# Hybrid encoder layer with 16 experts: the first expert gathered by itself, and its weights laid out block by block in the first ring slots

## The chip, the core and the metric

The kernel runs on one core of a Trainium2 chip. The metric is the device time of one execution in microseconds (us); the kernel before takes 1386.49 us as the median of 3 runs (1386.35 to 1389.76).

## What is computed

One encoder layer on 512 tokens of width 1024, all in float32: a trunk (an mLSTM branch and a differential attention branch, gated, projected and added to x), then a mixture of 16 experts in which each expert chooses its 64 best tokens, then a norm. The change lies at the seam between trunk and experts.

```python
def expert_choice_ffn(h, w_router, w_gate, w_up, w_down):
    cap = EC_CAPACITY * S // N_EXPERTS            # 64
    aff = jax.nn.softmax(jnp.einsum('bsd,de->bse', h, w_router), axis=-1)
    g, idx = lax.top_k(aff.transpose(0, 2, 1), cap)
    xe = h[bidx, idx]
    hid = (jax.nn.silu(jnp.einsum('becd,edf->becf', xe, w_gate))
           * jnp.einsum('becd,edf->becf', xe, w_up))
    ye = jnp.einsum('becf,efd->becd', hid, w_down) * g[..., None]
    return jnp.zeros_like(h).at[bidx, idx].add(ye)
```

Each expert has three weight matrices of 1024 x 2048 or 2048 x 1024, 8.39 MB each; the 16 experts have 402.7 MB.

## The kernel before

**The seam.** The trunk ends with the router and the choice of tokens: eight rounds of max and match-replace on VectorE (DVE) give each expert's threshold, two masks `gt_` and `eq_` (lines 931, 932) say which tokens are above or at it, and matmuls with a triangle of ones (`before`, lines 938 to 944) count how many chosen tokens stand ahead of each. The result is `slot` (line 948): the place of each token in each expert's list of 64. Dummy matmuls by `keep_warm` (line 159, `zps<-ident`) stand in the program's order on TensorE (PE): 28 beside the eight rounds, and `WARM2` = 7 ahead of the counting matmuls.

**Gather.** The 64 tokens of an expert are picked by a matmul with a one-hot matrix `ohr`, scaled by the token's norm. `gather(p)` does this for a pair of experts at once: per block of 128 features four matmuls (line 997) have `xn`, 128 x 128, as the stationary operand and 128 columns of `ohr` (64 of each expert) as the moving one. ScalarE (ACT) and DVE in turn bring the result from PSUM into `xe` (lines 1001, 999). A pair has 8 such blocks, b = 0 to 7. Before expert 0 the DVE makes `ohr` for the pair with three large operations (lines 983, 987); later pairs use small ones, half of them on GpSimd (POOL; line 991).

**An expert.** The gate pass and the up pass have 8 feature blocks each (line 1045, `pgate<-w,xe` and `pup<-w,xe`); a block is 4 matmuls of 512 columns, and reads 1 MB of weights. Then come Silu (ACT, line 1213), a product (DVE, line 1225), transposes of the hidden activations (`hid_T`, lines 1076 to 1080), and the down pass (line 1111). The order on PE and on SyncE (SP) is the program's: expert 0 does gate and up in turn, piece by piece, with the gather between (`first_up`); every expert e from 1 on does its gate pass, in which the transposes of expert e-1 lie (and, for an even e, the gather of its pair; for an odd e, the matrices of the scatter, lines 1016 and 1027), then the down pass of e-1, then its up pass.

**The weight ring.** Weights come through 11 slots of 2 MB (`mw`). The list `PIECES` says in which order: 192 pieces of 2 MB, that is two blocks of gate or up, or a quarter of a down matrix. SP issues one DMA per piece, in this order; a piece that goes into a used slot waits on SP until the PE has done the last matmul of the slot's old piece, and all later pieces wait behind it. The first 11 pieces (the 16 blocks of expert 0, and 6 of the 8 gate blocks of expert 1) are loaded beside the end of the trunk, as its tiles come free. Three slots are taken out of the ring for other data on their way (`keep`): the slot of expert 0's last up piece holds the scatter's matrices (`mats`). Piece n of the rest and its slot: 11 (expert 1, gate, last) in 0; 12 to 15 (expert 0, down) in 1 to 4; 16 and 17 (expert 1, up) in 5 and 6; 18 and 19 in 8 and 9; 20 (expert 2, gate, first) in 10; 21 in 0.

`sg` (activations of an expert) and `hT` (their transposes) are two tiles of 4 KB per partition of their own.

Of the kernel before, what the change touches and what calls it, by code (L numbers as in the profile page):

```python
# [9 lines left out]
F32 = mybir.dt.float32  # L10
# [8 lines left out]
P = 128  # L19
# [14 lines left out]
NG = 9  # L34
WARM0 = 30
WARM1 = 28
WARM2 = 7
NSLOT = 11

PIECES = [(0, m, j) for j in range(4) for m in ("gate", "up")]  # L40
PIECES += [(e, m, j) for s in range(1, NE + 1)
           for e, m in ((s, "gate"), (s - 1, "down"), (s, "up")) if e < NE
           for j in range(4)]


def _slots():

    keep = {(0, "up", 3): "mats", (1, "down", 3): "acc", (12, "gate", 0): "gf"}
    of, kept, old = list(range(NSLOT)), {}, 0
    for _ in range(NSLOT, len(PIECES)):  # L50
        while PIECES[old] in keep:
            kept[keep[PIECES[old]]] = of[old]
            old += 1
        of.append(of[old])
        old += 1
    return of, kept
# [6 lines left out]
def kernel(  # L63
# [869 lines left out]
    keep_warm(WARM2)  # L933
    cnt = [bank(t, (P, NT, NE)) for t in ("sc", "pv")]

    def before(c, m, first, last):
# [6 lines left out]
    for t in range(NT):  # L943
        pe.matmul(cnt[1], one, gt_[:, t:t + 1].broadcast_to([P, NT, NE]), start=(t == 0), stop=False)
    before(cnt[1], eq_, False, True)
    for i in range(2):
        ve.tensor_tensor(pl2[:, i], msk[:, i], cnt[i], op=OP.mult)
    ve.tensor_add(slot, pl2[:, 0], pl2[:, 1])
# [11 lines left out]

        return mw.tile([P, 4096], dtype, tag=f"w{KEPT[what]}", name=what)

    def slot_for(e, m, j):
        n = npiece[0]
        assert PIECES[n] == (e, m, j)
        npiece[0] += 1
        return mw.tile([P, 4096], F32, tag=f"w{SLOT_OF[n]}", name="w")

# [2 lines left out]

    xe = mm.tile([P, ND, 2 * CAP], F32, name="xe")
    ohr = mm.tile([P, NT, 2 * CAP], F32, name="ohr")
    sg = mm.tile([P, D], F32, name="sg")
    hT_ = mm.tile([P, ND, P], F32, name="hT")
    ga = consts.tile([P, 2, 1], F32, name="ga")
    fs = consts.tile([P, 6, NT], F32, name="fs")

    def gather(p):

        if p == 0:
            o4 = ohr.rearrange("p t (j c) -> p t j c", j=2)
            ve.tensor_tensor(o4, iota.unsqueeze(1).unsqueeze(1).broadcast_to([P, NT, 2, CAP]),
                             slot[:, :, 0:2].unsqueeze(3).broadcast_to([P, NT, 2, CAP]), op=OP.is_equal)
            for t in (0, 2):
                o = ohr[:, t:t + 2]
                ve.tensor_tensor(o, o, rst2[:, t:t + 2].unsqueeze(2).broadcast_to([P, 2, 2 * CAP]), op=OP.mult)  # L987
        for t in range(NT if p else 0):
            for j in range(2):
                e = 2 * p + j  # L990
                (gp if j else ve).tensor_scalar(ohr[:, t, j * CAP:(j + 1) * CAP], iota, slot[:, t, e:e + 1],
                                                rst2[:, t:t + 1], op0=OP.is_equal, op1=OP.mult)
        for b in range(ND):
            pg = pgt((P, 2 * CAP))
            c0 = 256 * (b // 2) + b % 2
            for t in range(NT):
                pe.matmul(pg, xn[t][:, c0:c0 + 255:2], ohr[:, t], start=(t == 0), stop=(t == NT - 1))  # L997
            if b % 2:
                ve.tensor_scalar(xe[:, b], pg, gff[:, b:b + 1], None, op0=OP.mult)
            else:  # L1000
                se.activation(xe[:, b], pg, AF.Copy, scale=gff[:, b:b + 1])  # L1001
            yield

    def scatter_mats(p):
# [27 lines left out]
    def up_bank(tag):  # L1032
        return pm.tile([P, 2, 512], F32, tag=tag, name=tag, bufs=1)

    def up_piece(e, m, w, j, pu, ahead, behind):
        half = (e % 2) * CAP
        wt = slot_for(e, m, j)
        sy.dma_start(wt, w[0, e, j * 256:(j + 1) * 256, :].rearrange("(p i) f -> p (i f)", i=2))
        for i in range(2):
            next(ahead, None)  # L1040
            b = 2 * j + i
            for c in range(2):
                for s in range(2):
                    c0 = i * DFF + s * D + c * 512
                    pe.matmul(pu[s * 64:(s + 1) * 64, c], xe[:, b, half:half + CAP], wt[:, c0:c0 + 512],  # L1045
                              start=(b == 0), stop=(b == ND - 1))
                next(behind, None)

    def up_pass(e, m, w, tag, ahead, behind):

        pu = up_bank(tag)
        next(ahead, None)
        for j in range(4):
            up_piece(e, m, w, j, pu, ahead, behind)
        for _ in behind:
            pass
        return pu

    def first_up():

        g, pg, pu = gather(0), up_bank("pgate"), up_bank("pup")
        next(g)
        next(g)
        for j in range(4):
            up_piece(0, "gate", w_gate_e, j, pg, nothing, nothing)
            up_piece(0, "up", w_up_e, j, pu, g, nothing)
        return pg, pu

    def hid_T():
# [135 lines left out]
    for e in range(NE + 1):  # L1205
        b = e - 1
        if e == 0:
            pg, pu = first_up()
        elif e < NE:
            pg = up_pass(e, "gate", w_gate_e, "pgate", nothing if e % 2 else gather(e // 2),  # L1210
                         chain(hid_T(), scatter_mats(b // 2) if e % 2 else nothing))
        if e < NE:
            se.activation(sg, pg.rearrange("p a b -> p (a b)"), AF.Silu)
        if 0 < e < NE:
            down(b)
        if e == NE:
            for _ in hid_T():
                pass
            last_down(b)
        else:  # L1220
            if e:
                pu = up_pass(e, "up", w_up_e, "pup", nothing, scatter(b // 2) if b % 2 else nothing)
# [40 lines left out]
```

## Time and profile before

| | |
|---|---|
| median of 3 runs | 1386.49 us |
| the profiled execution: its time, its span | 1386.85 us, 1384.8 us |
| PE busy | 1300.5 us, 94% |
| DVE, ACT, POOL busy | 412.6, 306.9, 120.8 us |
| bytes moved by DMA | 444.30 MB, mean 321 GB/s |
| mean granted TensorE clock | 0.993 of full speed |
| chain that ended last | PE 65%, DMA 29%, DVE 3%, ACT 2%, issue 1% |

The span runs from the first to the last instruction; the time of the execution has 2.05 us more around it. The trunk takes the first 455 us, the experts the rest. PE's busy share is high throughout, but PE is counted as busy while matmuls are pipelined; which engine sets the pace of the experts is read from the DMA's share and from PE's waits. "Chain that ended last" follows the last instruction back through whatever released each step.

### The profile page before, as it was taken

The page shows a single profiled execution, that of the slowest core. Times are in us where ns is not written, and L with a number is a line of the kernel's source. Part 1 is how long each engine was busy: PE and PEld are TensorE (multiplying, and loading weights), DVE is VectorE, ACT ScalarE, POOL GpSimd, SP SyncE. Part 2 cuts the span into 40 slices and gives each one's busy share as a digit, 9 for nine tenths or more (in the row PEclk, how much of TensorE's full clock was granted, in tenths as well). Part 3 has the DMA queues.
Part 4 walks back from the last instruction along what each step waited for, and adds up shares of the span by engine and source line. Part 5 has one row for each costly group of instructions (what it writes and reads, how often), then busy time and mean ns, then how long its engine had stood idle before and what let it go on. Part 6 is the DMA issues. An engine that isn't in the chain of part 4 may idle for free.

```text
span 1384.8 us, 16485 instructions
## 1 busy us (share of the span) xinstructions
PE 1300.5 (94%) x6762; PEld 723.6 (52%) x6762; DVE 412.6 (30%) x989; ACT 306.9 (22%) x634; POOL 120.8 (9%) x217
## 2 busy tenths in 40 slices
PE   8999999999999999999999997999899799889976
PEld 8988887888888434334333332423333242333435
DVE  5787759753344111111121020120112012001113
ACT  7676646433331010000000100000000000100003
POOL 3010312101201020000000000000000000000001
PEclk9999999999999999999999999999999999999998
DMA  7222242223488799999999999999999999999995
GB/s 202 63 77 77 77 107 61 77 76 106 129 327 344 276 415 430 425 430 428 426 428 428 427 429 425 428 428 428 429 426 428 427 429 427 428 428 428 426 403 178
DMA packets 84312, 444.30 MB, mean 321 GB/s; under 512 B 6176, under 2 KB 53350, under 8 KB 60174
## 3 DMA queue, kind: packets, MB, share of 16 engines
q1 hardware_dynamic: 81966, 438.95, 77.9%
q10 hardware_dynamic: 2240, 4.25, 1.2%
q8 instruction: 53, 0.87, 0.3%
q14 instruction: 21, 0.17, 0.0%
q0 software_dynamic: 32, 0.07, 0.0%
HBM read 441.10 MB, written 2.11 MB: 320 GB/s over the span
## 4 chain that ended last, share of the span: by engine, by line
PE 65%; DMA 29%; DVE 3%; ACT 2%; issue 1%; SPq 0%; DVEq 0%; ACTq 0%
DMA w<-in_w_up_e_dram 26%; PE pgate L1045 13%; PE pup L1045 10%; PE pd L1111 4%; PE zps L301 4%; PE zps L303 4%; PE zps L302 4%; PE pg L997 4%; PE pg L1098 3%; DMA w<-in_w_gate_e_dram 2%; PE pt L1076 1%; PE pn L582 1%; PE pa L1016 1%; PE bank L775 1%; PE zps L611 1%; PE zps L610 1%
## 5 line engine op out<-in xcount | busy, mean ns | idle before, releaser
L1045 PE MATMUL pup<-w,xe 128*64 128x512 f32 x1024 | 240.2, 601 | 35.7 <-DMA w<-in_w_up_e_dram 35.7
L1045 PE MATMUL pgate<-w,xe 128*64 128x512 f32 x1024 | 245.7, 605 | 0.3 <-DMA w<-in_w_gate_e_dram 0.3
L1111 PE MATMUL pd<-w,hT 128*64 128x512 f32 x896 | 198.1, 594 | 16.1 <-DMA w<-in_w_down_e_dram 16.1
L1045 PEld LDWEIGHTS pup<-w,xe 128*64 128x64 f32 x1024 | 65.6, 136 | 175.8 <-issue 114.1
L1111 PEld LDWEIGHTS pd<-w,hT 128*64 128x64 f32 x896 | 62.7, 137 | 149.2 <-issue 115.8
L1093 DVE SCALAR_TENSOR_TENSOR mats<-pd,ga,mats 64x512 fp32r<-64x512 f32 (+2 forms) x36 | 24.9, 690 | 329.2 <-ACT mats L1091 328.7
L1045 PEld LDWEIGHTS pgate<-w,xe 128*64 128x64 f32 x1024 | 64.4, 136 | 100.7 <-issue 88.8
L301 PE MATMUL zps<-hH,sp 128*128 128x512 f32 x256 | 102.0, 398 | 0.8 <-DVE hL L225 0.8
L303 PE MATMUL zps<-hH,sp 128*128 128x512 f32 x256 | 100.0, 391 | 0.0
L302 PE MATMUL zps<-hL,sp 128*128 128x512 f32 x256 | 99.8, 390 | 0.0
L241 DVE TENSOR_TENSOR sp<-raw,sp 128x512 fp32r<-128x512 f32 x114 | 78.1, 688 | 54.3 <-ACT sp L240 51.7
L997 PEld LDWEIGHTS pg<-ohr,xn 128*128 128x128 f32 x512 | 65.2, 198 | 46.5 <-issue 46.5
L240 ACT ACTIVATE sp<-raw 128x512 fp32r<-128x512 f32 x114 | 70.6, 629 | 69.3 <-PE zps L611 27.6
L997 PE MATMUL pg<-ohr,xn 128*128 128x128 f32 x512 | 75.9, 294 | 1.8 <-DVE ohr L987 1.8
L1091 ACT ACTIVATE mats<-pd,ga 64x512 fp32r<-64x512 f32 (+2 forms) x36 | 22.9, 635 | 220.6 <-PE pd L1111 196.9
L1225 DVE TENSOR_TENSOR sg<-sg,pup 128x512 f32<-128x512 f32 x32 | 20.6, 684 | 151.9 <-PE pup L1045 151.9
L1001 ACT ACTIVATE xe<-pg,gff 128x128 f32<-128x128 f32 x32 | 11.8, 367 | 233.5 <-PE pg L997 233.5
L1080 ACT ACTIVATE hT<-pt 128x512 f32<-128x512 f32 x16 | 9.6, 597 | 229.8 <-PE pt L1076 229.8
L1010 POOL TENSOR_SCALAR mats<-iota,slot 128x64 fp32r<-128x64 f32 x64 | 26.7, 444 | 335.6 <-PE pt L1027 328.4
L301 PEld LDWEIGHTS zps<-hH,sp 128*128 128x128 f32 x256 | 48.1, 188 | 10.6 <-POOL sp L275 1.0
L303 PEld LDWEIGHTS zps<-hH,sp 128*128 128x128 f32 x256 | 48.1, 188 | 10.4
L302 PEld LDWEIGHTS zps<-hL,sp 128*128 128x128 f32 x256 | 48.2, 188 | 9.5
(323 smaller groups left out, 1583.7 us busy)
## 6 DMA issues: line engine op xcount, KB each, us to landing
w<-in_w_gate_e_dram SPq DMA_DIRECT2D x64, 2048.0 KB
w<-in_w_up_e_dram SPq DMA_DIRECT2D x64, 2048.0 KB
w<-in_w_down_e_dram SPq DMA_DIRECT2D x60, 2048.0 KB
raw<-in_w_in_dram SPq DMA_DIRECT2D x44, 512.0 KB
raw<-in_w_out_dram SPq DMA_DIRECT2D x8, 512.0 KB
w<-in_w_down_e_dram SPq DMA_DIRECT2D x4, 1024.0 KB
x<-in_x_dram SPq DMA_DIRECT2D x4, 512.0 KB
mb<-mrow_d ACTq DMA_DIRECT2D x4, 512.0 KB
```

The source lines that it names most:

```text
L240: se.activation(sp[:, 0], raw, AF.Copy)
L241: ve.tensor_sub(sp[:, 1], raw, sp[:, 0].bitcast(F32))
L301: pe.matmul(zp, w[:, 1], hT(hH, k), start=(k == 0), stop=False)
L302: pe.matmul(zp, w[:, 0], hT(hL, k), start=False, stop=False)
L303: pe.matmul(zp, w[:, 0], hT(hH, k), start=False, stop=(k == ND - 1))
L997: pe.matmul(pg, xn[t][:, c0:c0 + 255:2], ohr[:, t], start=(t == 0), stop=(t == NT - 1))
L1010: (gp if j else ve).tensor_scalar(oa[:, t, j * CAP:(j + 1) * CAP], iota, slot[:, t, e:e + 1], None, op0=OP.is_equal)
L1045: pe.matmul(pu[s * 64:(s + 1) * 64, c], xe[:, b, half:half + CAP], wt[:, c0:c0 + 512], start=(b == 0), stop=(b == ND - 1))
L1091: se.activation(yb[r, 0, c], src[r], AF.Copy, scale=ga[r, e % 2])
L1093: ve.scalar_tensor_tensor(yb[r, 1, c], src[r], ga[r, e % 2], yb[r, 0, c].bitcast(F32), op0=OP.mult, op1=OP.subtract)
L1098: pe.matmul(pq, oaT[:, v, t], yb[:, i, cols], start=(i == 0), stop=(i == 1))
L1111: pe.matmul(pd[s * 64:(s + 1) * 64], hid_col(q, i), wt[:, i * D + hf * 512:i * D + (hf + 1) * 512], start=(c == 0), stop=(c == 15))
```

## The change

- The first 12 pieces are made of single blocks of 1 MB, two to a slot: (gate 0, up 0), (gate 1, up 1) ... (gate 6, up 6) of expert 0 in slots 0 to 6, then (gate 7 of expert 0, gate 0 of expert 1) in 7, and gate 1 and 2, 3 and 4, 5 and 6 of expert 1 in 8, 9 and 10. Piece 11 is gate 7 of expert 1, alone in slot 0. The slot kept for `mats` is 6. Up 7 of expert 0 goes into a 12th place: the 8 KB per partition of the tile `sh`, which after expert 0 holds `sg` and `hT`. SP issues one DMA of 1 MB for each of these 24 blocks.
- From piece 12 on the list is the old one. The slots of pieces 12 to 16 stay; 17 goes into slot 7 (before: 6); 18, 19, 20 and 21 stay in 8, 9, 10 and 0.
- `gather(0, (0,))` picks the tokens of expert 0 alone (64 moving columns), in the pass of expert 0; `gather(0, (1,))` those of expert 1, in the gate pass of expert 1. Expert 0's one-hot columns are made by four small DVE operations.
- Expert 0 does gate and up block by block: gather block b+1, gate b, up b.
- `WARM2` is 4, and these dummy matmuls come after the counting matmuls.

```diff
-WARM2 = 7
+WARM2 = 4
...
-PIECES = [(0, m, j) for j in range(4) for m in ("gate", "up")]
+BLOCKS = [(0, m, b) for b in range(8) for m in ("gate", "up")][:-1] + [(1, "gate", b) for b in range(8)]
+PIECES = [tuple(BLOCKS[n:n + 2]) for n in range(0, len(BLOCKS), 2)]
+NFIRST = len(PIECES)
...
-    keep = {(0, "up", 3): "mats", (1, "down", 3): "acc", (12, "gate", 0): "gf"}
+    keep = {PIECES[6]: "mats", (1, "down", 3): "acc", (12, "gate", 0): "gf"}
...
-    sg = mm.tile([P, D], F32, name="sg")
-    hT_ = mm.tile([P, ND, P], F32, name="hT")
...
+    for _ in range(NSLOT):
+        first_piece()
+    early[0, "up", 7] = mm.tile([P, DFF], F32, tag="sh", name="wsh", bufs=1)
+    weights(early[0, "up", 7], 0, "up", 7)
...
+    def gather(p, js=(0, 1)):
+
+        for j in js:
+            for t in range(NT):
                 e = 2 * p + j
                 (gp if j else ve).tensor_scalar(ohr[:, t, j * CAP:(j + 1) * CAP], iota, slot[:, t, e:e + 1],
                                                 rst2[:, t:t + 1], op0=OP.is_equal, op1=OP.mult)
+        js = slice(js[0] * CAP, (js[-1] + 1) * CAP)
...
-                pe.matmul(pg, xn[t][:, c0:c0 + 255:2], ohr[:, t], start=(t == 0), stop=(t == NT - 1))
+                pe.matmul(pg[:, js], xn[t][:, c0:c0 + 255:2], ohr[:, t, js], start=(t == 0), stop=(t == NT - 1))
...
-        g, pg, pu = gather(0), up_bank("pgate"), up_bank("pup")
+        g, pg, pu = gather(0, (0,)), up_bank("pgate"), up_bank("pup")
         next(g)
-        next(g)
-        for j in range(4):
-            up_piece(0, "gate", w_gate_e, j, pg, nothing, nothing)
-            up_piece(0, "up", w_up_e, j, pu, g, nothing)
+        for b in range(ND):
+            next(g, None)
+            up_block(0, b, early[0, "gate", b], pg)
+            up_block(0, b, early[0, "up", b], pu)
...
             pg, pu = first_up()
+            sh = mm.tile([P, 2 * D], F32, tag="sh", name="sh", bufs=1)
+            sg, hT_ = sh[:, 0:D], sh[:, D:].rearrange("p (a b) -> p a b", a=ND)
         elif e < NE:
-            pg = up_pass(e, "gate", w_gate_e, "pgate", nothing if e % 2 else gather(e // 2),
+            pg = up_pass(e, "gate", "pgate", gather(0, (1,)) if e == 1 else nothing if e % 2 else gather(e // 2),
                          chain(hid_T(), scatter_mats(b // 2) if e % 2 else nothing))
```

How the order on the engines changes, at three places. The first is PE at the end of the choice of tokens (`tk`: the thresholds, `tri` and `one`: triangle and square of ones, `msk`: the masks). Before:

```order
L927 MATMUL bank<-ident,tk 128x16
L159 MATMUL zps<-ident 128x128 x7
L938 LDWEIGHTS tri
L938 MATMUL bank<-msk,tri 128x64
...
L940 MATMUL bank<-msk,one 128x16
L997 MATMUL pg<-ohr,xn_3779 128x128
```

and now:

```order
L930 MATMUL bank<-ident,tk 128x16
L940 LDWEIGHTS tri
L940 MATMUL bank<-msk,tri 128x64
...
L942 MATMUL bank<-msk,one 128x16
L162 MATMUL zps<-ident 128x128 x4
L1011 MATMUL pg<-ohr,xn_3779 128x64
```

The dummy matmuls no longer stand ahead of the counting ones, and the gather has half the columns. The second place is PE in the gate pass of expert 1, from the last block of expert 0 (`pup`) to the down pass (`pd`). Before:

```order
L1045 MATMUL pup<-w,xe 64x512 x8
L1045 MATMUL pgate<-w,xe 64x512 x6
L1076 MATMUL pt<-ident,sg 128x128 x4
L1045 MATMUL pgate<-w,xe 64x512 x4
L1076 MATMUL pt<-ident,sg 128x128 x4
L1045 MATMUL pgate<-w,xe 64x512 x6
L1016 MATMUL pa<-aff,mats 128x2 x8
...
L1045 MATMUL pgate<-w,xe 64x512 x8
L1111 MATMUL pd<-w,hT 64x512 x32
```

and now its beginning (each gather is four rows of `L1011`, of which one is shown):

```order
L1054 MATMUL pup<-wsh,xe 64x512 x4
L1011 MATMUL pg<-ohr,xn_3779 128x64
...
L1054 MATMUL pgate<-w,xe 64x512 x4
L1011 MATMUL pg<-ohr,xn_3779 128x64
...
L1054 MATMUL pgate<-w,xe 64x512 x2
L1096 MATMUL pt<-ident,sh 128x128 x4
L1054 MATMUL pgate<-w,xe 64x512 x2
L1011 MATMUL pg<-ohr,xn_3779 128x64
...
L1054 MATMUL pgate<-w,xe 64x512 x8
L1131 MATMUL pd<-w,sh 64x512 x32
```

Eight gather blocks have come into this pass, two of them ahead of its first block. The third place is ACT at the end of expert 0. Before:

```order
L1001 ACTIVATE xe<-pg,gff 128x128 x4
L1213 ACT_TABLE_LOAD
L1213 ACTIVATE sg<-pgate 128x1024
L1080 ACTIVATE hT<-pt 128x512
```

and now:

```order
L1015 ACTIVATE xe<-pg,gff 128x64 x4
L1235 ACT_TABLE_LOAD
L1235 ACTIVATE sh<-pgate 128x1024
L1015 ACTIVATE xe<-pg,gff 128x64 x2
L1100 ACTIVATE sh<-pt 128x512
```

Behind the Silu now stands the `xe` of expert 1's first gather block; and the Silu writes the tile that held up 7, so the wait for the last matmul of that block stands ahead of the table load.

## Rows read from the trace of the kernel before

**Rows 1.** The page, busy tenths in 40 slices of 34.6 us:
```profile
PE   8999999999999999999999997999899799889976
DMA  7222242223488799999999999999999999999995
```
**Rows 2.** Windows: stretch, engines' busy us, clock, DMA share, GB/s.
```profile
455.00:469.00 14.00, 13.72 (x68) 7.27 (x70) 1.17 (x4) 0.73 (x2) 0.00 (x0) 0.88 0.40 144
469.00:510.00 41.00, 41.00 (x210) 17.27 (x206) 5.83 (x21) 4.55 (x7) 6.23 (x14) 1.00 0.98 401
510.00:530.00 20.00, 20.00 (x96) 6.75 (x94) 1.50 (x2) 2.67 (x4) 2.81 (x7) 1.00 1.00 417
530.00:1310.00 780.00, 732.86 (x3460) 278.01 (x3458) 110.44 (x228) 58.73 (x96) 33.75 (x72) 1.00 1.01 428
```
**Rows 3.** Timeline of SP's DMA issues: start, us, what (pieces 11, 20, 21).
```profile
462.61 0.33 SPq L1038 DMA_DIRECT2D w<-in_w_gate_e_dram  x1
...
509.10 0.33 SPq L1038 DMA_DIRECT2D w<-in_w_gate_e_dram  x1
...
513.27 0.33 SPq L1038 DMA_DIRECT2D w<-in_w_gate_e_dram  x1
```
**Rows 4.** Chain that ended last, from the thresholds to the first gate block.
```profile
451.36 1.76 PE zps L159 x14
...
453.25 0.46 DVE pl L947 x2
453.73 0.23 DVE slot L948
...
455.28 2.81 PE pg L997 x16
458.09 4.48 PE pgate L1045 x16
```
**Rows 5.** Timeline of DVE: the mask, and small one-hot operations of the next pair.
```profile
451.47 0.22 DVE L931 TENSOR_TENSOR msk<-aff,bank 128x64 bf16<-128x64 f32 x1 [0.39 <-PE bank L927]
...
484.94 0.79 DVE L991 TENSOR_SCALAR ohr<-iota,slot,rst 128x64 f32<-128x64 f32 x3 [8.39 <-PE pg L997]
```
**Rows 6.** Chain, expert 0's pass in its regular part: one period of 4 blocks.
```profile
468.58 3.43 PE pgate L1045 x16
472.01 1.14 PE pg L997 x8
473.15 1.87 PE pup L1045 x8
...
478.03 3.43 PE pgate L1045 x16
```
**Rows 7.** Chain, the gate pass of expert 1 and its end.
```profile
494.34 2.57 PE pgate L1045 x12
496.92 0.68 PE pt L1076 x4
...
502.86 1.88 PE pa L1016 x16
...
506.61 0.59 PE pt L1027 x4
...
513.23 13.73 PE pd L1111 x64
```
**Rows 8.** Timeline of ACT around the Silu of expert 0.
```profile
482.64 0.37 ACT L1001 ACTIVATE xe<-pg,gff 128x128 f32<-128x128 f32 x1 [9.08 <-PE pg L997]
483.02 1.28 ACT L1213 ACT_TABLE_LOAD   x1
490.95 1.02 ACT L1213 ACTIVATE sg<-pgate 128x1024 f32<-128x1024 f32 x1 [6.65 <-PE pgate L1045]
```
**Rows 9.** Windows of 1 us: granted clock is the third number from the end.
```profile
457.00:458.00 1.00, 1.00 (x6) 0.79 (x4) 0.00 (x0) 0.00 (x0) 0.00 (x0) 0.50 0.00 0
...
460.00:461.00 1.00, 1.00 (x6) 0.29 (x4) 0.00 (x0) 0.00 (x0) 0.00 (x0) 1.00 0.00 0
```

More of the change, by code (lines that the diff above doesn't have):

```diff
@@ L36 @@
 WARM1 = 28
-WARM2 = 7
+WARM2 = 4
 NSLOT = 11
-PIECES = [(0, m, j) for j in range(4) for m in ("gate", "up")]
+BLOCKS = [(0, m, b) for b in range(8) for m in ("gate", "up")][:-1] + [(1, "gate", b) for b in range(8)]
+PIECES = [tuple(BLOCKS[n:n + 2]) for n in range(0, len(BLOCKS), 2)]
+NFIRST = len(PIECES)
 PIECES += [(e, m, j) for s in range(1, NE + 1)
-           for e, m in ((s, "gate"), (s - 1, "down"), (s, "up")) if e < NE
+           for e, m in ((s, "gate"), (s - 1, "down"), (s, "up")) if e < NE and (e, m) != (1, "gate")
            for j in range(4)]
 def _slots():
-    keep = {(0, "up", 3): "mats", (1, "down", 3): "acc", (12, "gate", 0): "gf"}
+    keep = {PIECES[6]: "mats", (1, "down", 3): "acc", (12, "gate", 0): "gf"}
     of, kept, old = list(range(NSLOT)), {}, 0
@@ L932 @@
     ve.tensor_tensor(eq_, aff, taus, op=OP.is_equal)
-    keep_warm(WARM2)
     cnt = [bank(t, (P, NT, NE)) for t in ("sc", "pv")]
@@ L945 @@
     before(cnt[1], eq_, False, True)
+    keep_warm(WARM2)
     for i in range(2):
@@ L961, in kept, with slot_for @@
         return mw.tile([P, 4096], dtype, tag=f"w{KEPT[what]}", name=what)
-    def slot_for(e, m, j):
+    def slot_for(*key):
         n = npiece[0]
-        assert PIECES[n] == (e, m, j)
+        assert PIECES[n] == key
         npiece[0] += 1
@@ L973, with weights, first_piece @@
     ohr = mm.tile([P, NT, 2 * CAP], F32, name="ohr")
-    sg = mm.tile([P, D], F32, name="sg")
-    hT_ = mm.tile([P, ND, P], F32, name="hT")
+    def weights(wt, e, m, b, n=1):
+        w = (w_gate_e if m == "gate" else w_up_e)[0, e, b // 2 * 256:(b // 2 + 1) * 256, :]
+        sy.dma_start(wt, w.rearrange("(p i) f -> p (i f)", i=2)[:, b % 2 * DFF:(b % 2 + n) * DFF])
+    early = {}
+    def first_piece():
+        n = npiece[0]
+        wt = slot_for(*PIECES[n])
+        for i, key in enumerate(PIECES[n]):
+            early[key] = wt[:, i * DFF:(i + 1) * DFF]
+            weights(early[key], *key)
+    for _ in range(NSLOT):
+        first_piece()
+    early[0, "up", 7] = mm.tile([P, DFF], F32, tag="sh", name="wsh", bufs=1)
+    weights(early[0, "up", 7], 0, "up", 7)
     ga = consts.tile([P, 2, 1], F32, name="ga")
     fs = consts.tile([P, 6, NT], F32, name="fs")
[L979 to L989, printed above, removed]
+    def gather(p, js=(0, 1)):
+        for j in js:
+            for t in range(NT):
                 e = 2 * p + j
@@ L996, in gather @@
             for t in range(NT):
-                pe.matmul(pg, xn[t][:, c0:c0 + 255:2], ohr[:, t], start=(t == 0), stop=(t == NT - 1))
+                pe.matmul(pg[:, js], xn[t][:, c0:c0 + 255:2], ohr[:, t, js], start=(t == 0), stop=(t == NT - 1))
             if b % 2:
-                ve.tensor_scalar(xe[:, b], pg, gff[:, b:b + 1], None, op0=OP.mult)
+                ve.tensor_scalar(xe[:, b, js], pg[:, js], gff[:, b:b + 1], None, op0=OP.mult)
             else:
-                se.activation(xe[:, b], pg, AF.Copy, scale=gff[:, b:b + 1])
+                se.activation(xe[:, b, js], pg[:, js], AF.Copy, scale=gff[:, b:b + 1])
             yield
@@ L1033, in up_bank, with up_block, up_pass @@
         return pm.tile([P, 2, 512], F32, tag=tag, name=tag, bufs=1)
-    def up_piece(e, m, w, j, pu, ahead, behind):
+    def up_block(e, b, wt, pu, behind=nothing):
         half = (e % 2) * CAP
[L1037 to L1049, printed above, removed]
+        for c in range(2):
+            for s in range(2):
+                c0 = s * D + c * 512
+                pe.matmul(pu[s * 64:(s + 1) * 64, c], xe[:, b, half:half + CAP], wt[:, c0:c0 + 512],
+                          start=(b == 0), stop=(b == ND - 1))
+            next(behind, None)
+    def up_pass(e, m, tag, ahead, behind):
         pu = up_bank(tag)
         next(ahead, None)
-        for j in range(4):
-            up_piece(e, m, w, j, pu, ahead, behind)
+        for b in range(ND):
+            if (e, m) == (1, "gate"):
+                if npiece[0] < NFIRST:
+                    first_piece()
+                wt = early[e, m, b]
+            elif b % 2 == 0:
+                both = slot_for(e, m, b // 2)
+                weights(both, e, m, b, 2)
+                wt = both[:, 0:DFF]
+            else:
+                wt = both[:, DFF:]
+            next(ahead, None)
+            up_block(e, b, wt, pu, behind)
         for _ in behind:
@@ L1059, in first_up @@
     def first_up():
-        g, pg, pu = gather(0), up_bank("pgate"), up_bank("pup")
+        g, pg, pu = gather(0, (0,)), up_bank("pgate"), up_bank("pup")
         next(g)
-        next(g)
-        for j in range(4):
-            up_piece(0, "gate", w_gate_e, j, pg, nothing, nothing)
-            up_piece(0, "up", w_up_e, j, pu, g, nothing)
+        for b in range(ND):
+            next(g, None)
+            up_block(0, b, early[0, "gate", b], pg)
+            up_block(0, b, early[0, "up", b], pu)
         return pg, pu
@@ L1221 @@
             if e:
-                pu = up_pass(e, "up", w_up_e, "pup", nothing, scatter(b // 2) if b % 2 else nothing)
+                pu = up_pass(e, "up", "pup", nothing, scatter(b // 2) if b % 2 else nothing)
             for i in range(2):
```

## The prediction

> **What bounds the kernel now.** First the slices of the page [rows 1]: DMA stands at 9 from the 15th slice (485 us) to the 39th, while PE shows gaps from the 25th (830 us) on. So the weight stream sets the pace there, and it has no hole to its end. Then the windows [rows 2]: over the 780 us from 530 to 1310 it moves 428 GB/s, so a block of 1 MB (1.0486 MB) takes 2.45 us and a piece of 2 MB 4.9 us. Between 455 and 469 the mean is 144 GB/s: all 11 slots are full, so 22 blocks are in, and nothing more is asked for until PE gives a slot back. The first issue after that is at 462.61 [rows 3].
>
> So there is one number to watch: how many blocks have arrived by 530 us, from where the stream never stops. Before, these are 22 + (144 x 14 + 401 x 41 + 417 x 20) / 1048.6 = 22 + 25.56 = 47.56 [rows 2]. Each block more or less at 530 moves the end by 2.45 us, because the pieces that follow are the same in both kernels, and PE waits for them. The question is therefore not when expert 0 is done but when slots come free, and in which order.
>
> **How quickly slots come free.** Before, expert 0 has a period of 9.45 us (468.58 to 478.03) for 4 blocks [rows 6], that is two slots; the stream needs 9.8 us for them. The two are nearly matched, so from 469 to 530 the stream just runs (401 and 417 GB/s), and any delay of PE in this stretch is a delay of the stream. Of the period, a block takes 3.43 / 2 = 1.715, a gather block 1.14, and coming back from it 1.87 - 1.715 = 0.155 [rows 6]: a gather costs 1.295.
>
> **Edits, part by part.**
>
> *Warm-up moved.* On the chain the 7 dummy matmuls stand from 451.36 to 453.12 ahead of the counting [rows 4], though the mask begins at 451.47 and takes 0.22 [rows 5]. Now the counting begins at about 451.8, and `slot` is there about 1.0 earlier, at 452.95 instead of 453.96. One small one-hot operation (0.79 / 3 = 0.26 [rows 5]) takes the place of two large ones, so the gather begins about 453.35 instead of 455.28: 1.9 earlier. Four dummies (4/7 of 1.76 = 1.0) lie beside the DVE's work. The gather's first block is paced by four one-hot operations to 454.3, the second ends at 455.3. The first gate block begins at 455.35 instead of 458.09.
>
> *Clock.* Before, the granted clock falls to 0.50 (1.2 GHz) in the microsecond at 457 and is back at 1.00 (2.4 GHz) at 460 [rows 9], after PE stood idle up to 455.28. Two gather blocks took 2.81 instead of 2 x 1.14, and four blocks 4.48 instead of 3.43 + 0.155 [rows 4, 6]: 1.4 together. Now PE has work through the same stretch, and I take 2.4 GHz; the other end is 1.4 later.
>
> *Half the columns per gather.* No row has a gather of 64 columns. `pa` has the same 128 x 128 stationary tile and only 2 moving columns: 16 records in 1.88 [rows 7], so 8 take 0.94, against 1.14 with 128 columns. A gather of 64 costs between 0.94 and 1.14, with the return between 1.095 and 1.295; I take the middle, 1.2, since 64 lies halfway. Two of them cost 2.4 where one of 1.295 stood: gathering apart adds PE work. By contrast the Trainium skill, page "TensorE: Matmul & The Clock Gate", section "Step-by-step: what each phase is for", calls throughput "purely `N cycles`", one moving column per cycle. By that, a gather of 64 would be half of one of 128, and the sum would come out as in the second rival below.
>
> *Expert 0.* Slot 0 comes free after gate 0 and up 0: 455.35 + 0.155 + 3.43 = 458.95, against 462.57 before (458.09 + 4.48 [rows 4]). Each further slot takes 3.43 + 1.2 = 4.63: 463.6, 468.2, 472.8, 477.5, 482.1 for slots 1 to 5. Slot 6 is kept. Expert 0 ends at 455.35 + 0.155 + 16 x 1.715 + 6 x 1.2 = 490.15 instead of 494.34 [rows 7].
>
> *The 12th place.* Up 7 is one block more in stock. Its DMA waits for `slot` (452.95), and the stream has work up to about there, so it is in by 457. The 12 more issues on SP (0.33 each [rows 3]) are covered by the stream's own time; without that cover they would cost 4.
>
> *Silu.* The table load (1.28) and the Silu (1.02) now start at the end of up 7, and the `xe` of expert 1's first block (0.37) waits behind them [rows 8]: before, the table was loaded at 483.02, while PE worked. With 0.2 for three handovers (my estimate) the first gate block begins at 490.15 + 2.87 = 493.0. The two gather blocks ahead of it would be done by 492.2, so this wait costs 0.8; it lies on PE's path.
>
> *Gate pass of expert 1.* Before it takes 513.23 - 494.34 = 18.89 [rows 7]: 8 blocks 13.72, transposes 2 x 0.68, `pa` 1.88, `pt` 2 x 0.59, and 5 returns of 0.155. Now six gathers come in between (7.2; two were ahead), three of them right behind `pa` or `pt`, which saves returns. Its gates end at 493.0 + 0.155 + 13.72 + 7.2 + 4.42 + 2 x 0.155 = 518.8, not 513.23. Slot 7, which now waits for gate 0 of expert 1, comes free at 494.85. Slots 8, 9 and 10 each have two blocks, two gathers and a transpose pair, `pa` or a `pt` pair: 7.5, 7.7 and 7.0 more, so 502.35, 510.05, 517.1.
>
> **The sum.** A lone piece lands 6.6 after its issue: piece 11, issued at 462.61, has 2.02 of its 2.10 MB in at 469 [rows 2, 3]; that is 1.7 beyond 4.9. Block counts now: 23 at 457; piece 11 (one block) with slot 0; piece 12 issued at 463.6 makes 26 at 470.2; pieces 13 to 16 follow without a gap, 34 at 489.8. Then the stream runs dry: piece 17 waits for slot 7 (494.85) and makes 36 at 501.5, piece 18 makes 38 at 509.0, piece 19 makes 40 at 516.7. Piece 20 is issued at 517.15, against 509.10 [rows 3], and from 517.15 + 1.7 = 518.85 the stream goes on for good, since piece 21 follows slot 0 (518.8) and each down piece needs 3.43 on PE (13.73 / 4 [rows 7]) against 4.9. At 530 there are 40 + 11.15 / 2.45 = 44.55 blocks instead of 47.56. The 3.0 missing cost 7.4 us. In one line: expert 0 ends 4.2 earlier; the gate pass of expert 1, from 490.15 to 518.8, is 9.8 longer; and slot 10, with gates 5 and 6 instead of 4 and 5, comes free 1.7 before its end instead of 4.1: 8.0 later. Of that the stream's own lag before (piece 20 waited for its turn a little) takes back 0.6.
>
> The profiled execution took 1386.85, 0.36 above the median; so 1394.25 on its scale and **1393.9** on the median's. Alone, this forecast reaches from 1391.4 (gathers at 1.095: -1.3; Silu hidden: -0.8; handovers and lag -0.4) to 1396.8 (gathers at 1.295: +1.1; clock +1.4; handovers and lag +0.4).
>
> **Rivals.** 1. *The early slots stay ahead* (faster). If from piece 12 on the stream never ran dry, it would have 24 blocks at 465.3 and 24 + 64.7 / 2.45 = 50.4 at 530: 2.85 more than before, 7.0 us, 1379.5. For it speaks the hole of [rows 2], which is certainly shortened. It decides at slots 7 to 10: they would have to come free by 489.8, 494.7, 499.6 and 504.5. My releases are 5.0 to 12.6 later, and two gathers and a Silu stand ahead of the first. 8%.
>
> 2. *Gathers cost by their columns* (no change). At 1.14 / 2 = 0.57, with the return 0.725, twelve gathers on the path of slot 10 give back 5.7 and the second one at the start 0.45: slot 10 at 510.95, 47.06 blocks at 530, 1.2 us, 1387.7. Against it stands `pa`, where 2 columns cost more than four fifths of 128 [rows 7]. It decides if a gather of 64 takes under 0.7. The rule of the page named above is this case. 10%.
>
> 3. *The clock falls all the same* (slower still). The gather's first block is paced by DVE, so PE is not full there; 1.4 as above: 1395.3. It changes no sign. 25%, my own forecast 57%.
>
> **Chances.** Runs of this kernel tell 0.3% (4.2 us) from no change, so slower is over 1390.7: my forecast and the third rival, 0.82. Same 0.10, faster 0.08. The range takes my own span and, on the low side, comes down to the second rival: 1387.5 to 1397.5. Left out are the first rival and some of the third.
>
> **What would show it.** Right: first gate block near 455.4; piece 11 issued near 459; DMA idle from about 490 to 496, and lone pieces up to 517; piece 20 issued near 517; a gather of 64 columns at 0.94 to 1.14 for 8 records; table load and Silu behind up 7, and PE waiting for ACT there. Wrong: no dip in the DMA's share between 490 and 517, or piece 20 issued before 511. Then the releases of slots 7 to 10, or the gather's price, are misjudged.

## The result, and the profile after

The changed kernel takes 1396.2 us (median of 5 runs, 1394.75 to 1398.95), the kernel before, in 5 runs beside it on the same chip, 1388.68 (1386.35 to 1389.76). The ratio is 1.0062, 95% interval 1.0045 to 1.0080: slower by 6 to 11 us, as forecast (1393.9 against 1386.49 is a ratio of 1.0053). The ratios here and below leave out executions in a slower state, of which there was one (3882.69 us, one of the twelve of the run warm).

The slices of the page, PE and DMA, against [rows 1]: the DMA is busier in the 14th slice, and the dip has moved into the 15th, which was full before.

```profile
PE   8999999999999999999999998999899799889976
...
DMA  6222232223488869999999999999999999999994
```

The windows of [rows 2] for the kernel after (engines' busy time, granted clock, DMA share, GB/s):

```profile
455.00:469.00 14.00, 13.94 (x79) 7.07 (x79) 1.36 (x6) 0.63 (x2) 2.35 (x4) 1.00 0.70 222
469.00:510.00 41.00, 40.37 (x222) 20.02 (x219) 5.38 (x18) 4.36 (x8) 3.43 (x8) 1.00 0.83 329
510.00:530.00 20.00, 20.00 (x98) 8.32 (x99) 1.47 (x7) 2.53 (x4) 5.53 (x12) 0.91 0.79 295
530.00:1310.00 780.00, 731.55 (x3442) 275.90 (x3438) 111.25 (x226) 58.21 (x95) 33.65 (x72) 1.00 1.01 428
```

The hole at 455 to 469 became smaller (222 GB/s against 144), but the next two stretches fell from 401 and 417 to 329 and 295. From 530 on both kernels run at 428. So the change gives back later, and more, what it wins at the start.

The number that the prediction watches, blocks arrived by 530, follows from the same 75 us in both traces, counted from the mask (before, then after; why the second begins 2.04 later is told next):

```profile
455.00:530.00 75.00, 74.72 (x368) 31.30 (x370) 8.50 (x27) 7.96 (x12) 9.04 (x20) 0.98 0.88 358
457.04:532.04 75.00, 74.37 (x388) 34.23 (x388) 7.42 (x27) 7.20 (x13) 9.27 (x21) 0.98 0.80 305
```

That is (358 - 305) x 75 / 1048.6 = 3.8 blocks fewer, where the prediction has 3.0. At 2.45 us each they are 9.3 us; the ratio gives 8.6, the two medians 7.5.

One thing must be taken off first. This profiled execution took 1398.95, 2.75 above its median, and it was late before the change begins: the mask, at 451.47 before [rows 5], stands at 453.51 here. These 2.04 us belong to the trunk: in the traces of the runs below the mask stands anywhere from 450.97 to 453.41, with either layout of the weights. All times of after are compared below with 2.04 taken off. The chain that ended last, from the mask to the second period of expert 0:

```profile
453.51 0.23 DVE msk L934
...
454.25 1.01 PE zps L162 x8
...
455.31 2.10 PE pg L1011 x16
457.40 1.87 PE pgate L1054 x8
459.27 1.72 PE pup L1054 x8
460.99 1.09 PE pg L1011 x8
462.07 1.87 PE pgate L1054 x8
```

Two gather blocks take 2.10 instead of 2.81, and the first gate block begins at 457.40 - 2.04 = 455.36 (458.09 before [rows 4]). The clock is at 1.00 all through 455 to 469. A period of two blocks and a gather is 462.07 - 457.40 = 4.67.

The same chain around expert 0's end, and through the gate pass of expert 1:

```profile
490.72 1.74 PE pup L1054 x8
...
492.52 1.28 ACT L1235
...
493.82 1.02 ACT sh L1235
494.84 0.21 ACT xe L1015
...
495.10 1.94 PE pgate L1054 x8
497.03 1.09 PE pg L1011 x8
...
507.55 1.88 PE pa L1030 x16
509.43 1.10 PE pg L1011 x8
510.53 3.39 PE pgate L1054 x8
...
514.51 0.89 PE pg L1011 x8
515.40 1.87 PE pgate L1054 x8
...
518.74 3.58 PE pgate L1054 x16
522.32 3.00 PE pd L1131 x13
```

Expert 0 ends at 492.47. Then ACT loads the table and does the Silu, the gathered tokens wait behind both, and the gates of expert 1 run from 495.10 to 522.32, with six gathers among them. One row is nowhere in the forecast: the gate block at 510.53 takes 3.39, and the others 1.87 to 1.94. The windows there, PE alone, with the clock as the third number from the end:

```profile
510.00:511.00 1.00, 1.00 (x6) 0.58 1.07 459
511.00:512.00 1.00, 1.00 (x4) 0.50 0.27 115
512.00:513.00 1.00, 1.00 (x4) 0.50 0.04 16
513.00:514.00 1.00, 1.00 (x5) 0.71 0.00 0
514.00:515.00 1.00, 1.00 (x11) 1.00 0.68 115
```

The clock fell to 0.50 (1.2 GHz) while the profile shows PE busy without a gap. The last two columns are the stream's: from 512 to 514 next to nothing moves, until piece 19 is issued at 513.97, when the slow block gives back slot 9. The slow block made this hole longer but did not open it: in the run clk below, where no block is slow, the stream falls to 49 GB/s at 511 as well. SP's issues of pieces 11, 17, 19 and 20 answer to [rows 3]:

```profile
461.03 0.33 SPq L981 DMA_DIRECT2D w<-in_w_gate_e_dram  x1
...
497.07 0.33 SPq L981 DMA_DIRECT2D w<-in_w_up_e_dram  x1
...
513.97 0.33 SPq L981 DMA_DIRECT2D w<-in_w_up_e_dram  x1
...
520.65 0.33 SPq L981 DMA_DIRECT2D w<-in_w_gate_e_dram  x1
```

Piece 11 is early (458.99 on the scale of before, against 462.61), piece 20 late (518.61 against 509.10).

### The profile page after: what moved, and what is told of

Same layout as the page of the kernel before. It is cut to its first block, busy times and chain, and to the rows that moved or that the text cites. A ratio compares the mean times of both kernels' runs of the same rounds, so it can differ in the third digit from the quotient of the medians.

```text
span 1396.9 us, 16642 instructions
## 1 busy us (share of the span) xinstructions
PE 1311.5 (94%) x6820; PEld 731.3 (52%) x6820; DVE 413.4 (30%) x994; ACT 307.9 (22%) x638; POOL 122.3 (9%) x221
## 4 chain that ended last, share of the span: by engine, by line
PE 64%; DMA 29%; DVE 4%; ACT 2%; issue 1%; SPq 0%; DVEq 0%; ACTq 0%
DMA w<-in_w_up_e_dram 26%; PE pgate L1054 13%; PE pup L1054 10%; PE pd L1131 4%; PE pg L1011 4%; PE zps L304 4%; PE zps L306 4%; PE zps L305 4%; PE pg L1118 3%; DMA w<-in_w_gate_e_dram 2%; PE pt L1096 1%; PE pd L1178 1%; PE pn L585 1%; PE pa L1030 1%; PE bank L778 1%; PE bank L780 1%
## 5 line engine op out<-in xcount | busy, mean ns | idle before, releaser
L1131 PE MATMUL pd<-w,sh 128*64 128x512 f32 x896 | 198.1, 594 | 15.8 <-DMA w<-in_w_down_e_dram 15.8
L1131 PEld LDWEIGHTS pd<-w,sh 128*64 128x64 f32 x896 | 62.7, 137 | 148.8 <-issue 116.2
L1011 PEld LDWEIGHTS pg<-ohr,xn 128*128 128x128 f32 x576 | 72.7, 196 | 48.1 <-issue 46.2
L1011 PE MATMUL pg<-ohr,xn 128*128 128x128 f32 (+1 forms) x576 | 83.8, 291 | 0.1
L1015 ACT ACTIVATE xe<-pg,gff 128x128 f32<-128x128 f32 (+1 forms) x36 | 12.8, 355 | 237.2 <-PE pg L1011 237.2
L1247 DVE TENSOR_TENSOR sh<-sh,pup 128x512 f32<-128x512 f32 x32 | 20.6, 684 | 146.1 <-PE pup L1054 146.1
L1100 ACT ACTIVATE sh<-pt 128x512 f32<-128x512 f32 x16 | 9.6, 597 | 226.5 <-PE pt L1096 226.5
```

The lines of the kernel that those rows point to most:

```text
L1011: pe.matmul(pg[:, js], xn[t][:, c0:c0 + 255:2], ohr[:, t, js], start=(t == 0), stop=(t == NT - 1))
L1131: pe.matmul(pd[s * 64:(s + 1) * 64], hid_col(q, i), wt[:, i * D + hf * 512:i * D + (hf + 1) * 512], start=(c == 0), stop=(c == 15))
```

## The experiments

The theory is that of the prediction: until about 517 us the stream waits for slots, so PE's work ahead of a slot's release delays the end by its own length, and the gathers of expert 1 in its gate pass are that work. The rivals: the new layout (blocks of 1 MB, order of slots, shared space) is to blame; or the stream has a stock that hides PE's work. Ten runs follow (in the code shown, `...` stands for further lines); the kernel before was run beside each, and the ratios are to it.

### The parts, each alone

**split**: the kernel before, with the separate gather alone (`gather` itself is that of the change).

```diff
-        g, pg, pu = gather(0), up_bank("pgate"), up_bank("pup")
+        g, pg, pu = gather(0, (0,)), up_bank("pgate"), up_bank("pup")
...
-            pg = up_pass(e, "gate", w_gate_e, "pgate", nothing if e % 2 else gather(e // 2),
+            pg = up_pass(e, "gate", w_gate_e, "pgate", gather(0, (1,)) if e == 1 else nothing if e % 2 else gather(e // 2),
```

> The kernel before with one thing of the change alone: the first expert gathered alone in its own pass, the second in its own gate pass. Pieces, slots, sg and warm-up are those of before. Theory (the split gather is the whole loss): the gate pass grows by 7 to 8 us for six gathers, and by another 1.5 if the clock falls after pa; the Silu's table is loaded early as before; piece 21 is issued near 520 instead of 513.3, and the time is 4.5 to 8 above before, 1393 to 1396. Rival (the split matters little alone, the loss needs the new layout): within 2 of before.

Measured: 1395.46 us, ratio 1.0066 (1.0053 to 1.0078). This part alone costs as much as the whole change; the first theory holds, though the 8.6 us above the kernel before are a little more than the 4.5 to 8 expected. Its chain has the slow gate block at the same place, behind `pa` and a gather, although nothing of the layout is in it:

```profile
507.58 1.88 PE pa L1010 x16
509.46 0.99 PE pg L991 x8
510.45 3.26 PE pgate L1039 x8
```

**warm**: the kernel before, with the warm-up moved alone.

```diff
-    keep_warm(WARM2)
     cnt = [bank(t, (P, NT, NE)) for t in ("sc", "pv")]
...
     before(cnt[1], eq_, False, True)
+    keep_warm(WARM2)
```

> The kernel before with one thing of the change alone: four dummy matmuls behind the counting instead of seven ahead of it. Theory (PE's pace sets the stream until 517): the first gate block comes 1.0 earlier by the order alone and 1.4 earlier again if the dip of the clock at 457 goes; all slots come free that much earlier, and the end is 1.0 to 2.7 earlier: 1384 to 1387.5. If the dip stays, 1.0 at most. Rival (the stream is bound by itself from 469 on): no difference, within 0.5.

Measured: 1384.93 us, ratio 0.9989 (0.9979 to 0.9998): 0.3 to 2.9 us gained. The interval lies below 1, but its end does not exclude the rival, which allowed 0.5. The trace speaks for the theory: the mask comes 1.43 later than in before (452.90 against 451.47 [rows 5]), and yet piece 20 is issued at 507.73 against 509.10, so 2.8 earlier on the same scale.

**pair**: the changed kernel without the separate gather; the three large one-hot operations are back as well.

```diff
-        g, pg, pu = gather(0, (0,)), up_bank("pgate"), up_bank("pup")
+        g, pg, pu = gather(0), up_bank("pgate"), up_bank("pup")
...
-            pg = up_pass(e, "gate", "pgate", gather(0, (1,)) if e == 1 else nothing if e % 2 else gather(e // 2),
+            pg = up_pass(e, "gate", "pgate", nothing if e % 2 else gather(e // 2),
```

> The changed kernel with the gather of both experts of the first pair put back into expert 0's pass (128 columns a block, the three large one-hot operations), and nothing in the gate pass of expert 1. Layout of the pieces, 12th place and moved warm-up stay. Theory (the second expert's gathers in the gate pass hold back slots 7 to 10): the gate pass falls from 29.9 to about 19 to 20 us, piece 20 is issued near 508 to 510 (on the scale of the profiled execution of before), no lone pieces after about 506, about 48 blocks at 530: 1383 to 1387 us, 9 to 13 less than the changed kernel. Rival (the 1 MB transfers or the new order of the slots are to blame): the time stays above 1391, with holes in the DMA's share although the gate pass is short.

Measured: 1391.66 us, ratio 1.0038 (1.0026 to 1.0050). It is faster than the changed kernel, as the theory said, but above the 1387 that it allowed; the rival, which said over 1391, was right that the layout costs something too. Piece 20 is issued at 515.07, or 513.13 on the scale of before, and not at 508 to 510. The chain shows where (expert 0's end):

```profile
491.77 1.74 PE pup L1061 x8
...
493.56 1.28 ACT L1242
...
494.86 1.03 ACT sh L1242
...
495.94 4.49 PE pgate L1061 x12
```

`sg` now lies where up 7 lies, so table load and Silu follow up 7, and the gate pass of expert 1 needs the bank that the Silu reads. PE stands still from 493.51 to 495.94, 2.4 us, and then the clock falls (0.50 in the windows from 497 to 500): twelve records of `pgate` take 4.49 instead of 2.57 [rows 7]. In the changed kernel two gathers filled this hole, so that PE's idle time before the gate block is 0.63 there.

### The price of the layout

**pairsilu**: pair, with up 3 in the 12th place instead of up 7, and the table loaded early.

```diff
-BLOCKS = [(0, m, b) for b in range(8) for m in ("gate", "up")][:-1] + [(1, "gate", b) for b in range(8)]
+BLOCKS = [(0, m, b) for b in range(8) for m in ("gate", "up")]
+BLOCKS.remove((0, "up", 3))
+BLOCKS += [(1, "gate", b) for b in range(8)]
...
             next(g, None)
+            if b == 6:
+                se.activation(fs[:, 5, 0:1], xe[:, 6, 0:1], AF.Silu)
             up_block(0, b, early[0, "gate", b], pg)
```

> The kernel of the run pair, with two things more: the 12th place holds up 3 in place of up 7, so that the space of sg is free long before the Silu, and a Silu of one column behind the last xe of expert 0 loads the table there. Theory (what kept pair 4.8 above before is the Silu that waits for up 7: 2.4 of idle PE, and the clock that falls after it): PE goes from up 7 to the next gate pass without a gap, the clock stays at 1.00, three halves of the gate pass take 2.58 instead of 4.49, and the time falls by 4 to 4.5 against pair, to 1387 to 1388. Rival A (the 12th place is worth its block of 2.45 once it costs no wait): 1384 or less, below the run warm. Rival B (1 MB transfers or the order of the slots cost by themselves): still above 1390.

Measured: 1389.09 us, ratio 1.0013 (1.0003 to 1.0023). The gate pass now follows up 7 without a gap (490.78 + 1.72), and its first twelve records take 2.58:

```profile
492.50 2.58 PE pgate L1063 x12
```

So the two edits at the Silu together were worth 0.25% of the 0.49% between pair and warm, 3.5 us. Rival A falls: the block in stock does not pay here. Rival B (still above 1390) is not met; against transfers of 1 MB as a cause also stands that all of the 24 but piece 11's are issued before 453, though no run changes the size alone. Against warm 0.24%, 3.3 us, are left (the forecast of 1387 to 1388 was a little low). PE is only in part to blame. The gate passes begin at 492.50 here and at 492.97 in warm, but the masks stand at 450.97 and 452.90, so on one scale this one begins 1.46 later: its first two gathers ran at a lower clock (3.58 against 2.12). That is less than the stream lost: from 470 to 510 this kernel moves 362 GB/s and warm 411:

```profile
470.00:510.00 40.00, 40.00 (x206) 17.17 (x206) 5.83 (x21) 5.04 (x8) 8.10 (x18) 1.00 0.95 362
```

The same window of warm:

```profile
470.00:510.00 40.00, 40.00 (x206) 17.01 (x204) 5.90 (x21) 4.83 (x7) 7.51 (x17) 1.00 1.00 411
```

These 49 GB/s are 1.9 blocks. A slot comes free only when both of its blocks are used, in either layout; in the new one slot 7 holds a block of each expert, and piece 11 puts one block into slot 0. Piece 17, which waits for slot 7, is issued at 494.26, in warm (slot 6) at 489.58, on one scale 6.6 earlier. That suggests half-empty slots.

**half**: warm, with piece 11 cut into two pieces of one block, a slot each; each later piece thus waits for the next slot's release.

```diff
+PIECES[11:12] = [(1, "gate", 3, 0), (1, "gate", 3, 1)]
...
+        if (e, m, j) == (1, "gate", 3):
+            wts = [slot_for(e, m, j, i) for i in range(2)]
+            for i in range(2):
+                sy.dma_start(wts[i][:, i * DFF:(i + 1) * DFF],
+                             w[0, e, 768:1024, :].rearrange("(p i) f -> p (i f)", i=2)[:, i * DFF:(i + 1) * DFF])
```

> The kernel of the run warm, with the last gate piece of expert 1 cut into two blocks of 1 MB that take a slot each, half of it empty. Theory A (what the new layout still costs in the run pairsilu are slots with one block in them, a block of stock less from there to the gates' end): pieces 12 to 21 are asked for one release later, the stream stands still for about a block in the gate pass, and the time is 1.5 to 3.5 above warm. Theory B (stock does not matter, only when PE is done): within 1 of warm.

Measured: 1389.86 us, ratio 1.0021 (1.0011 to 1.0031), 0.32% or 4.4 us above warm by the ratios. Half-empty slots cost, so theory B falls; the size is above the 1.5 to 3.5 expected (the two intervals together leave 1.8 to 7.2). Most of it shows at once, since the first slot now brings one block: 460 to 475 moves 203 GB/s against 309 in warm, 1.5 blocks or 3.7 us less. That the 3.3 us left in pairsilu have this cause is argued from its slots 0 and 7, not shown: no run has the new layout with full slots.

### Does PE's work count wherever it stands?

**twice**: warm, with both experts gathered separately, all in expert 0's pass.

```diff
+    def both():
+        g0, g1 = gather(0, (0,)), gather(0, (1,))
+        for n in range(ND):
+            next(g0)
+            if n > 1:
+                next(g1)
+            yield
...
-        g, pg, pu = gather(0), up_bank("pgate"), up_bank("pup")
+        g, pg, pu = both(), up_bank("pgate"), up_bank("pup")
```

> The kernel of the run warm, with both experts of the first pair gathered by themselves (64 columns each), but both in expert 0's pass: sixteen gather blocks there in place of eight, none in the gate pass of expert 1. PE does 8 blocks of 1.09 more, less 0.05 on each of the others: some 8.3 us. Theory A (until about 517 the stream waits for slots, so PE's work ahead of a release counts wherever it stands): the time is 6.5 to 8.5 above warm, 1391.5 to 1394. Theory B (only the gate pass of expert 1 is tight, the stock covers work in expert 0's pass): at most 3 above warm, 1388 or less.

Measured: 1392.38 us, ratio 1.0035 (1.0023 to 1.0047), 7.45 above warm's median and 0.46% (6.4 us) by the ratios. Theory A: the eight blocks more cost their own length in expert 0's pass as well. The gates of expert 1 begin here 47.06 after the mask (453.14), in warm 40.07 (492.97 - 452.90), 7.0 later, and piece 20 is issued 7.0 later too:

```profile
500.20 2.58 PE pgate L1039 x12
```

**pamove**: the counter-test, PE work taken out of the gate pass. `pa` and the two `pt` groups (1.88 + 2 x 0.59 on PE) go into expert 0's down pass, where PE has time to spare.

```diff
-                         chain(hid_T(), scatter_mats(b // 2) if e % 2 else nothing))
+                         chain(hid_T(), scatter_mats(b // 2) if e % 2 and e > 1 else nothing))
...
     def down(e):
         odd = e % 2
+        mats_of = scatter_mats(0) if e == 0 else nothing
...
+                for _ in range({0: 1, 9: 1, 11: 2, 13: 2, 15: 1}.get(c, 0)):
+                    next(mats_of, None)
```

> The kernel of the run warm, with the pa and pt products of the first pair moved from the gate pass of expert 1 into the down pass of expert 0. Theory (until about 515 the stream waits for slots, and PE's work ahead of a release delays it by its own length): gates 4 to 7 of expert 1 are done 1.9 to 3.1 earlier, pieces 20 and 21 are issued as much earlier, and the time falls by 1 to 3 against warm, to 1382 to 1384. The same work in the down pass costs nothing, since there a piece needs 3.4 on PE against 4.9 on the stream. Rival (the stream has enough in stock there, only the gathers' place decides): 1384.5 to 1385.5, as warm.

Measured: 1383.88 us, ratio 0.9969 (0.9957 to 0.9981): 0.20% or 2.8 us below warm by the ratios. Piece 20 is issued at 504.58 and piece 21 at 508.01, that is 12.00 and 15.43 after the gates of expert 1 began (492.58); in warm it is 507.73 and 511.90, 14.76 and 18.93 after (492.97). So the releases come 2.8 and 3.5 earlier: the length of `pa` and of the `pt` groups that stood ahead of each, with the returns. This is faster than the kernels before and after.

**best**: pamove, with `mats` in the slot of expert 1's last gate piece, so that the releases from piece 18 on move up by one.

```diff
-    keep = {(0, "up", 3): "mats", (1, "down", 3): "acc", (12, "gate", 0): "gf"}
+    keep = {(1, "gate", 3): "mats", (1, "down", 3): "acc", (12, "gate", 0): "gf"}
...
-            if e == 0:
-                mats = kept("mats", F32R)
...
+        if e == 1:
+            mats = kept("mats", F32R)
```

> The kernel of the run pamove, with the constants' place (mats) taken from the slot of the last gate piece of expert 1 instead of the slot of the last up piece of expert 0, so that from piece 18 on each piece is asked for one slot release earlier. Theory (slot releases in the gate pass set the stream): piece 18 is issued with the end of expert 0, no hole between 490 and 515, and the time falls by 1.5 to 4 more, to 1379 to 1382.5. Rival (the stream has no hole left there): as pamove within 0.7.

Measured: 1384.59 us, ratio 0.9976 (0.9967 to 0.9985): as pamove, the theory's gain is not there. The window from 465 to 530 shows why little was left to win, 416 GB/s:

```profile
465.00:530.00 65.00, 65.00 (x322) 25.44 (x320) 7.33 (x23) 7.23 (x10) 9.07 (x20) 1.00 1.00 416
```

The same of pamove:

```profile
465.00:530.00 65.00, 65.00 (x320) 25.41 (x322) 7.75 (x24) 7.22 (x10) 8.95 (x20) 1.00 0.99 412
```

Here the stream already ran nearly through (428 is its rate later), and earlier releases were worth nothing that shows; what remains is mainly the hole before 465 (128 GB/s from 455 on).

### The price of a gather, and the clock

**cols**: the changed kernel, with all 128 columns in each gather of expert 1.

```diff
+        full = js if js.start == 0 else slice(0, 2 * CAP)
...
-                pe.matmul(pg[:, js], xn[t][:, c0:c0 + 255:2], ohr[:, t, js], start=(t == 0), stop=(t == NT - 1))
+                pe.matmul(pg[:, full], xn[t][:, c0:c0 + 255:2], ohr[:, t, full], start=(t == 0), stop=(t == NT - 1))
```

> The changed kernel, with 128 moving columns in each gather of expert 1 in its gate pass in place of 64 (both halves are computed, one is used). If a gather is paid by its stationary tiles, eight records take 1.14 instead of 1.09 (0.89 to 0.95 or so behind pt), and the gate pass grows by under 1. If it is paid by its moving columns, a block takes twice as long as in the changed kernel, and the gate pass grows by 6 or more.

Measured: 1397.64 us in one run; the reading is that of the chain:

```profile
496.24 1.14 PE pg L1012 x8
...
506.92 1.88 PE pa L1031 x16
508.80 1.05 PE pg L1012 x8
509.84 1.87 PE pgate L1055 x8
...
512.30 0.94 PE pg L1012 x8
```

Twice the columns cost 1.14 instead of 1.09, and 0.94 instead of 0.89 behind `pt`. So here a gather is paid by its records and hardly by its columns. And the gate block at 509.84 takes 1.87: with 128 columns the clock did not fall.

**clk**: the changed kernel, with the gather behind `pa` done one block earlier.

```diff
-            next(ahead, None)
+            for _ in range(1 if e != 1 else 2 if b == 3 else 0 if b == 4 else 1):
+                next(ahead, None)
             up_block(e, b, wt, pu, behind)
```

> The changed kernel with one gather block of expert 1 moved from behind pa to ahead of the gate block before it; PE does the same work. Theory A (the fall of the clock at 510 comes from pa and the gather following each other, three us with 2 and 64 moving columns): the granted clock stays at 1.00 there, eight records of pgate take 1.87 instead of 3.39, pieces 19 to 21 are issued 1.5 earlier, and the time is 1.5 less. Theory B (the clock falls at that point whatever stands there, or after the two gathers that now follow each other): a window of 0.50 to 0.66 remains in the gate pass, and the time is the same within 0.5.

Measured: 1393.38 us, ratio 1.0054 (1.0042 to 1.0066) against 1.0062 (1.0045 to 1.0080) for the changed kernel. The times go the way of theory A but don't tell the two apart; the trace does:

```profile
505.36 1.87 PE pgate L1054 x8
507.23 1.88 PE pa L1030 x16
509.11 1.87 PE pgate L1054 x8
```

No block of this gate pass is slow (two gather blocks, 2.03, stand ahead of these rows), and the clock stays at 1.00 from 495 to 530. Piece 20 is issued at 517.70, 65.46 after the mask (452.24), against 67.14 in after: 1.7 earlier, for 1.5 expected.

## Why the prediction was right, step by step

With 2.04 taken off the profiled times of after, the steps stand so:

| step | predicted | measured |
|---|---|---|
| first gate block | 455.35 | 455.36 |
| gather of 64 columns | 0.94 to 1.14 | 1.09 |
| period per slot | 4.63 | 4.67 |
| piece 11 issued | 458.95 | 458.99 |
| expert 0 ends | 490.15 | 490.43 |
| gates of expert 1 begin | 493.0 | 493.06 |
| PE waits there for the Silu's chain | 0.8 | 0.63 |
| piece 17 issued | 494.85 | 495.03 |
| piece 18 issued | 502.35 | 502.60 |
| piece 19 issued | 510.05 | 511.93 |
| gates of expert 1 end | 518.8 | 520.28 |
| piece 20 issued | 517.15 | 518.61 |

Up to piece 18 all steps are within 0.3. The start of the gates hides two misses that cancel: expert 0 ends 0.28 late, and the chain of table load, Silu and `xe` takes 2.63 instead of 2.87, because the `xe` of 64 columns takes 0.21 instead of 0.37 and the three handovers 0.1 instead of 0.2 (the prediction's own estimate, from no row). **The mis-sized term** is the gate pass of expert 1: predicted 28.65 with its Silu, measured 522.32 - 492.47 = 29.85. The prediction took 2.4 GHz throughout ("13.72" for eight blocks); one block at 3.39 instead of 1.87 costs 1.52 (the rest is 0.3 shorter, most of it the Silu's chain), and the end of the pass and piece 20 are late by 1.48 and 1.46. With these 1.5 us the forecast's ratio of 1.0053 would have been 1.0064 (1.5 / 1387 = 0.11%), beside the 1.0062 measured; but only one execution of this kernel has a trace, the longest of the five, and whether the clock fell in the others is not known. That the medians differ by 7.5 us, next to the 7.4 forecast, is in part luck. That the term is a clock's and not PE's work is shown by the windows (0.50), and by clk and cols, where the same block takes 1.87.

**The number watched**, blocks arrived by 530, holds beyond this kernel. Counted as above in the traces of the ten kernels that have a ratio, the blocks missing or gained against before, at 2.45 us each, give the time of the ratio within 1.3 us in eight (clk 7.5 and 7.5, pair 4.7 and 5.3, pairsilu 2.3 and 1.8), and within 2.4 in split (6.8 and 9.2) and pamove (1.9 and 4.3 gained).

**The first rival** (early slots stay ahead) is out: the DMA moves 98 GB/s between 495 and 500 in the trace of after, at the place where it had to run through (PE alone; the last number):

```profile
495.00:500.00 5.00, 4.90 (x26) 1.00 0.41 98
```

The runs show more: pairsilu has the early slots and no gather in the gate pass, and even so it isn't faster than before.

**The second rival** (columns) is out by 1.09 for 64 columns and by cols. The Trainium skill, page "TensorE: Matmul & The Clock Gate", section "Step-by-step: what each phase is for", has throughput as "purely `N cycles`". No run here agrees for these float32 gathers: 64 columns take 96% of the time of 128 (1.09 / 1.14).

**The third rival** (the clock falls all the same) has its place wrong in this execution: the gather at 455.31 runs at 1.00. But in the traces of pamove and pairsilu, which have the same warm-up, two gather blocks took 3.56 and 3.58 at the start instead of the 2.10 to 2.12 of the other eight. In pamove:

```profile
453.67 3.56 PE pg L997 x16
```

So the gain of 1.4 from the moved warm-up shows in some traces and not in others; why is not known. The interval of warm's gain, 0.3 to 2.9, leaves both the 1.0 and the 2.7 open.

**What the prediction did not split up**: it put the loss on the gathers in the gate pass. split shows that these alone cost 0.66%, as much as the whole. The layout's own price (pair against warm, 0.49%) overlaps with it, since the gathers fill the wait for the Silu: the parts (split, warm, layout) sum to 0.66 - 0.11 + 0.49 = 1.04%, the whole is 0.62%. Of the 0.42% in between (5.8 us), idle time and slow clock at the Silu explain (2.43 - 0.63) + 1.9 = 3.7; the rest is within the intervals and stays open.

The table load measured 1.28, and the Silu began 0.01 after it. The Trainium skill, page "ScalarE: Activation LUTs", section "What ACT_TABLE_LOAD costs", gives 1283 ns, which agrees, and a drain of about 1380 ns more, which shows neither ahead of the load (it began 0.05 after PE's last matmul) nor behind it. By an estimate from the drain of the Trainium skill the gates of expert 1 would have begun about 1.4 later than they did.

## What to carry to other kernels

Where a stream waits for buffers, look at the order in which they come free and count arrived blocks at the point from where the stream never stops again: what is loaded early is lost again if the stream runs dry later. Up to there, a microsecond of work ahead of a release cost about a microsecond in this kernel, whichever pass held it (twice, 7.0 us on PE and 6.4 in time), and work moved behind the last tight release gave its length back (pamove, 2.8 of 3.06). A buffer comes back when its last block is used, so a buffer half full is a block of stock less (half), and one shared by two stages comes back late (slot 7, argued from pairsilu's piece 17); and a place lent out for weights makes whoever owns it later wait for them.

## What was not expected of the hardware

The granted clock fell to 0.50 while PE was busy without a gap: after 1.88 of `pa` (2 moving columns) followed at once by a gather of 64 columns, in the traces of after and of split, and it was back after about 3 us. It did not fall when the gather had 128 columns (cols) nor when a gate block stood between them (clk), nor in the trace of before, where a gate block follows `pa` at once. These are one trace each, and at the start of the experts kernels with the same order differ (pamove, pairsilu), so what makes the clock fall stays open. After 2.4 us of idle PE (pair) it fell as well. An early block of weights in stock, which looks like pure gain, did not show as one (pairsilu).
